# A hybrid attention layer on one Trainium2 core: attention products tied to the emission order of the projection products

## The chip, the cores and the metric

The kernel runs on one core of one Trainium2 chip. The core has a matrix engine (PE, TensorE), three engines for elementwise work (DVE, VectorE; ACT, ScalarE; POOL, GpSimd) and a queue that issues the transfers between memory on and off the chip (SP, SyncE). Each engine takes its instructions in the order in which they stand in the built program. The metric is the time of one execution on the device in microseconds, taken as the median over several runs.

## What is computed

One encoder layer for 1024 positions of width 1024, in float32. A conditioning vector gives shifts, scales and gates. Two groups of eight heads attend side by side, latent attention (MLA) and attention over a band of nine chunks (CA), and a gated MLP follows.

```python
mod = jnp.dot(jax.nn.silu(c), w_ada[l]) + b_ada[l]
sh_a, sc_a, g_a, sh_m, sc_m, g_m = jnp.split(mod, N_MOD, axis=-1)
h = modulate(rmsnorm(x, g_attn_norm[l]), sh_a, sc_a)
proj = jnp.dot(h, w_in[l])
q_lat, kv_lat, k_rope, ca_qkv = jnp.split(proj, split_pts, axis=-1)
q = jnp.dot(rmsnorm(q_lat, g_q_latent[l]), w_q_up[l])
kv = jnp.dot(rmsnorm(kv_lat, g_kv_latent[l]), w_kv_up[l])
...
o_mla = mla_attention(q, k, v)
o_ca = chunk_attention(cq, ck, cv, rel_bias[l])
mixed = jnp.dot(jnp.concatenate([o_mla, o_ca], axis=-1), w_out[l])
x = x + g_a[:, None, :] * mixed
h = modulate(rmsnorm(x, g_mlp_norm[l]), sh_m, sc_m)
u = causal_dwconv(jnp.dot(h, w_up[l]), conv_w[l], conv_b[l])
gate, val = jnp.split(u, 2, axis=-1)
x = x + g_m[:, None, :] * jnp.dot(jax.nn.silu(gate) * val, w_down[l])
```

## The kernel before

A float32 product is made as three products of high and low parts (`gemm3`). The stages are: the normed input, its transposes and the first query and key projection (qk0); the attention stage, in which all other projections and both kinds of attention run side by side; the output projection and the preparation of the MLP; the MLP up, with its convolution; the MLP down. The change touches the attention stage alone.

The attention stage emits two streams of work. The first is the attention itself: 16 CA units (4 head pairs, 2 heads, 2 halves of the queries) and then 16 MLA units. A unit n is worked on in pieces:

- `prep` turns the unit's queries and keys on PE (`turned`, tag T, one PSUM buffer) and ACT and DVE write them as 16-bit high and low pages; it is done two units ahead.
- `guard(j)` (L755, L763) makes the scores of 128 queries once, only to take their extreme with a DVE reduction (L771); `mrow` turns these into a row that is added to the scores later. Both are done one unit ahead.
- `st(x)` (L815) makes the scores of key block x, transposed; ACT takes the exponential (L819), ACT or POOL its high half (L823, L77), DVE the low half (L826).
- `val(x)` (L841 to L843) multiplies these with the values, two blocks later (`DEPTH`), into one PSUM tile for the unit; after the last block ACT and DVE scale the result (L848 to L850) and SP stores it (L851).

The second stream is the filler: generators that make the other projections in the order v0, qk1, qk2, v1, qk3, m, up0, up1, oca. v and qk are the CA values, queries and keys, m the MLA latents, up0 and up1 the latents' projections to heads, oca the output projection of the CA half. `pace` advances the filler by one step for so much attention work. A step of `gemm3_f` (L162) is two pairs, that is six matmuls, or fewer at the end. Its weights come through `load_w` (L177): 16 tiles hold two sets of weights, three raw buffers receive the loads (L188), ACT makes the high half (L75), POOL the low half (L82). For v1 ACT also takes the squares of the raw weights (L191) into a scratch (tag sq, two buffers) that the norm of the queries and keys (L421) uses too. A side stream, `f_ada`, loads blocks of w_ada (L490) and sums them on DVE (L494); it is advanced with the filler and stores three of its gates through a DMA (L504) that waits for ACT's copy (L503).

What is emitted first does not run first: a scheduler places the instructions of each engine when the program is built, by priority and by when it takes their inputs to be ready. `tc.high_priority(offset=...)` raises a block's priority: 400 for prep, guards, rows and scores, 200 for values. `tc.issue_after(ins)` makes every instruction that its block puts on the engine of `ins` stand behind `ins` in that engine's order. It adds no wait on a semaphore. The kernel before uses it in one direction: a filler step stands behind the attention product that was emitted `LAG + 1` entries back (`trail`, to which every guard, score and value block adds its last matmul).

```python
trail.append(last.ins)
...
if len(trail) > LAG:
    with tc.issue_after(trail[-1 - LAG]):
        gemm3(pt, part, i0 == 0, i0 + step >= n)
```

Of the kernel before, what the change touches and what calls it, by code (L numbers as in the profile page):

```python
# [34 lines left out]
HD = 64  # L35
NM = QR + KVR + ROPE
GRP = 2
GSTEP, LAG = 2, 4
DEPTH = 2
OFF_S, OFF_V = 400, 200  # L40
TB = 1
# [21 lines left out]
def layer_kernel(ctx, tc, I, out):  # L63
    nc = tc.nc
    pe, act, dve, pool, sp = nc.tensor, nc.scalar, nc.vector, nc.gpsimd, nc.sync
# [84 lines left out]
    def gemm3(pt, pairs, start=True, stop=True):  # L150

        n = len(pairs)
        for i, (sh, sl, mh, ml) in enumerate(pairs):
            pe.matmul(pt, sh, mh, start=(start and i == 0), stop=False)
            pe.matmul(pt, sh, ml, start=False, stop=False)
            pe.matmul(pt, sl, mh, start=False, stop=(stop and i == n - 1))

    trail = []  # L160

    def gemm3_f(pt, pairs, step=GSTEP):  # L162
        n, w = len(pairs), pt.shape[-1]
        for i0 in range(0, n, step):
            part = pairs[i0:i0 + step]
            if len(trail) > LAG:
                with tc.issue_after(trail[-1 - LAG]):
                    gemm3(pt, part, i0 == 0, i0 + step >= n)
            else:
                gemm3(pt, part, i0 == 0, i0 + step >= n)  # L170
            yield 3 * len(part) * max(107, w / 2.4 + 2.5)


# [188 lines left out]
    for d in range(ND):  # L362
# [11 lines left out]
        for t in range(NT):  # L374
            h, j = divmod(t, 4)
            sl = slice(j * P, (j + 1) * P)
# [347 lines left out]
    class Unit:  # L724
# [14 lines left out]
        def guard(u, j):  # L739
            i = 4 * u.g + j  # L740
            lo = max(0, i - 4) if u.band else 0
            n = (i - lo + 1) * P
            n0 = max(0, min(4, i + 1) - lo) * P
            n1 = n - n0
            c0 = 512 - n0 if n1 else 0
            segs = [(c0, lo * P, n0, 0)] if n0 else []
            if n1:
                segs.append((512, max(lo, 4) * P - 512, n1, 1))
            q = slice(j * P, (j + 1) * P)
            rows = P if u.band else QK  # L750
            with tc.high_priority(offset=OFF_S):
                s = ps.tile([P, 1024], F32, name=f"s{u.nm}_{i}", tag="S", bufs=1)
                last = None
                for x, (c, ko, w, kh) in enumerate(segs):
                    last = pe.matmul(s[:, c:c + w], u.q[:rows, 0, q], kpages[u.nm, kh][:rows, 0, ko:ko + w],  # L755
                                     start=True, stop=True)
                if u.band:
                    bg = biases[u.hd][0]
                    w = min(n, 256)
                    pc = [(c0 + n - w, 256 - w, w)] if (n1 == 0 or n1 >= 256) else \  # L760
                        [(c0 + n - 256, 0, 128), (c0 + n - 128, 128, 128)]
                    for c, bo, w in pc:
                        last = pe.matmul(s[:, c:c + w], identr[:], bg[:, bo:bo + w], start=False, stop=True,  # L763
                                         skip_group_check=True)
                trail.append(last.ins)
                if u.band:
                    if i >= 4:
                        dve.memset(s[64:128, c0:c0 + 64], BIG)
                else:
                    dve.memset(s[0:64, c0 + n - 64:c0 + n], BIG)  # L770
                dve.tensor_reduce(mz[:, QK + j:QK + j + 1], s[:, c0:c0 + n], axis=AX.X, op=MIN)  # L771
            return sum(w / 2.4 + 12 for _, _, w, _ in segs) + (110 if u.band else 0)

        def mrow(u):
            r = u.row
            with tc.high_priority(offset=OFF_S):
                pt = turned(lambda j: mz[:, QK + j - r:QK + j + 1], r + 1, f"mr{u.nm}_{u.g}")
                act.activation(u.q[r:r + 1, u.slot], pt[r:r + 1], AF.Copy, scale=-1.0)  # L778
            return 4 * 110

        def st(u, x):
            b, t0, t1 = u.blocks[x]
            w = (t1 - t0 + 1) * P
            kt = u.kpage(b)
            kc = slice((b % 4) * P, (b % 4 + 1) * P)
            qc = slice((t0 - 4 * u.g) * P, (t0 - 4 * u.g) * P + w)
            nm = f"{u.nm}_{u.g}_{b}"
            r = u.row
            with tc.high_priority(offset=OFF_S):
                if u.first and x == 0:  # L790
                    pool.memset(f32(mk_k[32:33, 0:64]), 0.0)
                    pool.memset(f32(mk_k[0:1, 64:128]), BIG)
                s = ps.tile([P, 512], F32, name=f"t{nm}", tag="ST", bufs=2)
                todo = []
                if u.band:
                    todo.append((0, w, kt[:, 0, kc], u.q[:, 0, qc]))
                    todo.append((0, w, kt[:r + 1, 1, kc], u.q[:r + 1, 1, qc]))
                    if b >= t0:
                        bt = biases[u.hd][1]
                        wb = min(256, w)  # L800
                        todo += [(0, wb, identr[:], bt[:, a, :wb]) for a in range(2)]
                    elif b + 1 >= t0:
                        bt = biases[u.hd][1]
                        todo += [(0, P, identr[:], bt[:, a, P:2 * P]) for a in range(2)]
                    if t1 == b + 4:
                        todo.append((w - P, w, mk_k[:], mk_q[:]))
                else:
                    todo.append((0, w, kt[:r + 1, 0, kc], u.q[:r + 1, 0, qc]))
                    todo.append((0, w, kt[:r, 0, kc], u.q[:r, 1, qc]))
                    todo.append((0, w, kt[:r, 1, kc], u.q[:r, 0, qc]))  # L810
                    if b >= t0:
                        todo.append((0, P, mk_k[:], mk_q[:]))
                todo.append(todo.pop(1))
                for y, (c0, c1, l, m) in enumerate(todo):
                    last = pe.matmul(s[:, c0:c1], l, m, start=(y == 0), stop=(y == len(todo) - 1))  # L815
                trail.append(last.ins)
                ninv = (sca if u.band else scm)[:, 1:2]
                p = at.tile([P, 512], F32, name=f"p{nm}", tag="P", bufs=2)
                act.activation(p[:, :w], s[:, :w], AF.Exp, scale=ninv)  # L819
                hl = at.tile([P, 2, 512], F16, name=f"hl{nm}", tag="HL", bufs=HL_BUFS)  # L820
                cnt[0] += 1
                if HI_ON[cnt[0] % len(HI_ON)] == "a":
                    act.activation(hl[:, 0, :w], s[:, :w], AF.Exp, scale=ninv)  # L823
                else:
                    hi_of("p", hl[:, 0, :w], p[:, :w])
                dve.tensor_tensor(hl[:, 1, :w], p[:, :w], hl[:, 0, :w], op=SUB)  # L826
                u.hl[x] = hl
            return sum(max(107, (c1 - c0) / 2.4 + 12) for c0, c1, _, _ in todo)

        def val(u, x):  # L830
            b, t0, t1 = u.blocks[x]
            w = (t1 - t0 + 1) * P
            c = slice((t0 - 4 * u.g) * P, (t0 - 4 * u.g) * P + w)
            v, y = u.vst(b)
            w1, w2 = (v[:, y, a, u.odd:u.odd + 2].rearrange("p c b -> p (c b)") for a in range(2))
            hl = u.hl.pop(x)
            with tc.high_priority(offset=OFF_V):
                if x == 0:
                    u.pv = ps.tile([P, 512], F32, name=f"pv{u.nm}_{u.g}", tag="pv", bufs=1)
                end = x == len(u.blocks) - 1  # L840
                pe.matmul(u.pv[:, c], w1, hl[:, 0, :w], start=(x == 0), stop=False)  # L841
                pe.matmul(u.pv[:, c], w1, hl[:, 1, :w], start=False, stop=False)
                last = pe.matmul(u.pv[:, c], w2, hl[:, 0, :w], start=False, stop=end)  # L843
                trail.append(last.ins)
                if end:
                    ri = at.tile([P, 512], F32, name=f"ri{u.nm}_{u.g}", tag="ri", bufs=1)
                    r0, r1 = (slice(64, 128), slice(0, 64)) if u.odd else (slice(0, 64), slice(64, 128))
                    act.activation(ri[r0], u.pv[r1], AF.Ln)  # L848
                    act.activation(ri[r0], ri[r0], AF.Exp, scale=-1.0)
                    dve.scalar_tensor_tensor(ri[r0], u.pv[r0], vscale[u.vs][1][r0], ri[r0], op0=MUL, op1=MUL)  # L850
                    sp.dma_start(u.dst_d[:, u.g * 512:(u.g + 1) * 512], ri[r0])  # L851
            return 3 * (w / 2.4 + 3)
# [429 lines left out]
```

## Time and profile before

| | us |
|---|---|
| median of 3 runs | 1508.36 |
| lowest and highest of them | 1503.86, 1509.09 |
| the profiled execution's own time | 1507.0 |
| its span, from the first to the last instruction | 1505.2 |
| PE, DVE, POOL, ACT busy in that span | 1323.0, 1011.6, 818.5, 715.4 |

The profile is of one execution. Rows of stretches give for each engine how long it was busy and, after an x, how many instructions it ran, then the granted clock of PE as a share of full speed, the busy share of the DMA engines and their rate. Rows of groups give line, engine, operation, output and inputs with shapes, the count, the busy time in us and the mean of one in ns, and behind the bar the engine's idle time just before them with what ended it. Rows of events give start and duration in us. A matmul's duration in an event row includes its passage through the array, so that successive ones overlap; what counts is the distance of their starts.

### The profile page before, as it was taken

How to read it: one execution, taken by the hardware profiler on the slowest of the kernel's cores; microseconds unless marked ns; L12 is line 12 of the kernel's file. 1: busy time of each engine (PE TensorE's matmuls, PEld its weight loads, DVE VectorE, ACT ScalarE, POOL GpSimd, SP SyncE). 2: the span in 40 equal slices, each digit the busy share in tenths (PEclk: the TensorE clock that was granted, in tenths of full speed). 3: DMA queues.
4: the chain of work that ended last, by engine and by line, in shares of the span. 5: the costliest groups of instructions: out<-in, count | busy, mean ns of one | idle time of the engine just before them, and what ended most of it. 6: DMA issues, size and time to landing. Idle time of an engine off the chain costs nothing.

```text
span 1505.2 us, 19968 instructions
## 1 busy us (share of the span) xinstructions
PE 1323.0 (88%) x6926; PEld 1054.2 (70%) x6926; DVE 1011.6 (67%) x1421; ACT 715.4 (48%) x1319; POOL 818.5 (54%) x901
## 2 busy tenths in 40 slices
PE   3769999898868899988928759999999999999997
PEld 2769879776745556655716648888888887887885
DVE  8926665555667866565676668777777888666563
ACT  5435565454756766665453324444444433333331
POOL 5764444353698443322867245555556554665662
PEclk9979999999977999999958979999999999999999
DMA  8421223221110023324521142222222234446442
GB/s 308 124 67 50 64 61 111 80 74 43 57 35 8 18 82 98 103 81 149 211 98 56 56 154 84 85 84 84 78 77 84 85 123 172 147 145 231 163 140 98
DMA packets 80001, 153.02 MB, mean 102 GB/s; under 512 B 8214, under 2 KB 44314, under 8 KB 79900
## 3 DMA queue, kind: packets, MB, share of 16 engines
q1 hardware_dynamic: 79900, 151.75, 30.5%
q8 instruction: 54, 0.88, 0.3%
q14 instruction: 47, 0.39, 0.1%
HBM read 122.88 MB, written 28.84 MB: 101 GB/s over the span
## 4 chain that ended last, share of the span: by engine, by line
PE 34%; DVE 18%; POOL 16%; DMA 16%; issue 10%; ACT 5%; DVEq 0%; SPq 0%; POOLq 0%; ACTq 0%
DMA aw<-w_ada 7%; POOL wds L82 4%; DMA wu<-w_up 4%; PE tm L815 3%; DVE u L1132 3%; PE dnp L1196 2%; PE dnp L1197 2%; PE dnp L1198 2%; PE p L1126 2%; PE p L1124 2%; PE p L1125 2%; DVE aacc L494 2%; DVE wu L1154 2%; DVE u L1133 2%; DVE adaw L369 1%
## 5 line engine op out<-in xcount | busy, mean ns | idle before, releaser
L82 POOL TENSOR_TENSOR wds<-wd,wds 128x512 fp32r<-128x512 f32 x88 | 152.9, 1756 | 100.2 <-ACT wds L75 100.2
L75 ACT ACTIVATE wds<-wd 128x512 fp32r<-128x512 f32 x88 | 54.6, 624 | 152.2 <-PE dnp L1198 149.6
L1196 PE MATMUL dnp<-wds,g 128*128 128x512 f32 x308 | 119.7, 390 | 2.3 <-DVE c L1158 1.5
L1186 DVE TENSOR_TENSOR wd<-wd,gmbc 128x1024 f32<-128x1024 f32 x44 | 69.9, 1588 | 76.3 <-DMA wd<-w_down 76.2
L1198 PE MATMUL dnp<-wds,g 128*128 128x512 f32 x308 | 118.5, 390 | 2.2 <-DVE g L82 2.2
L1197 PE MATMUL dnp<-wds,g 128*128 128x512 f32 x308 | 119.7, 389 | 0.0
L82 POOL TENSOR_TENSOR wc<-ws,wc 128x512 fp32r<-128x512 f32 x22 | 55.4, 2520 | 74.2 <-ACT wc L75 74.2
L494 DVE SCALAR_TENSOR_TENSOR aacc<-aw,cs,aacc 128x256 f32<-128x256 f32 x84 | 45.4, 541 | 62.5 <-DMA aw<-w_ada 62.1
L82 POOL TENSOR_TENSOR wa<-wu,wa 128x512 fp32r<-128x512 f32 x22 | 36.7, 1669 | 90.6 <-ACT wa L75 90.6
L815 PE MATMUL tm<-qt,kt 96*128 96x512 f16 (+7 forms) x288 | 74.1, 346 | 7.7 <-ACT qt L778 4.7
L826 DVE TENSOR_TENSOR hlm<-pm,hlm 128x512 f16<-128x512 f32 (+1 forms) x96 | 58.3, 615 | 32.6 <-POOL hlm L77 17.8
L1132 DVE SCALAR_TENSOR_TENSOR u<-c,pk,u 128x1023 f32<-128x1023 f32 x44 | 75.5, 1724 | 4.1 <-ACT u L1131 4.1
L82 DVE TENSOR_TENSOR g<-gr,g 128x512 fp32r<-128x512 f32 x44 | 70.6, 1607 | 9.9 <-ACT g L75 9.9
L819 ACT ACTIVATE pc<-tc,sca 128x512 f32<-128x512 f32 (+3 forms) x96 | 50.2, 524 | 47.5 <-DVE hlc L826 27.9
L815 PEld LDWEIGHTS <-kt 128*128 128x128 f16 (+2 forms) x480 | 47.4, 102 | 35.2 <-issue 16.8
L77 POOL TENSOR_SCALAR hlm<-pm 128x384 f16<-128x384 f32 (+2 forms) x48 | 24.8, 516 | 82.9 <-ACT pm L819 65.1
L1196 PEld LDWEIGHTS dnp<-wds,g 128*128 128x128 f32 x308 | 57.8, 188 | 15.6 <-ACT wds L75 1.9
L1198 PEld LDWEIGHTS dnp<-wds,g 128*128 128x128 f32 x308 | 57.8, 188 | 15.0 <-DVE g L82 3.0
L819 ACT ACTIVATE pm<-tm,scm 128x512 f32<-128x512 f32 (+1 forms) x96 | 55.3, 579 | 27.2 <-PE tm L815 20.6
L1131 ACT ACTIVATE u<-c,pk 128x1024 f32<-128x1024 f32 x44 | 52.3, 1236 | 32.9 <-DVE c L1164 32.9
L826 DVE TENSOR_TENSOR hlc<-pc,hlc 128x512 f16<-128x512 f32 (+3 forms) x96 | 52.8, 553 | 22.5 <-POOL hlc L77 11.9
L1197 PEld LDWEIGHTS dnp<-wds,g 128*128 128x128 f32 x308 | 57.8, 188 | 11.9
(432 smaller groups left out, 4703.1 us busy)
## 6 DMA issues: line engine op xcount, KB each, us to landing
wu<-w_up SPq DMA_DIRECT2D x44, 512.0 KB, 3.5
wd<-w_down SPq DMA_DIRECT2D x44, 512.0 KB, 3.6
aw<-w_ada SPq DMA_DIRECT2D x96, 128.0 KB, 2.1
g_d<-u SPq DMA_DIRECT2D x22, 512.0 KB, 2.6
gr<-g_d SPq DMA_DIRECT2D x44, 256.0 KB, 2.8
x<-x SPq DMA_DIRECT2D x16, 512.0 KB, 7.1
adaw<-w_ada_a SPq DMA_DIRECT2D x16, 512.0 KB, 5.1
wq_r<-w_qk SPq DMA_DIRECT2D x32, 128.0 KB, 2.4
```

The costliest lines, as they stand in the source:

```text
L75: act.activation(o, i, AF.Copy)
L82: (pool if eng == "p" else dve).tensor_tensor(o, i, f32(hi), op=SUB)
L494: dve.scalar_tensor_tensor(acc[:], w[:], cs[:, k:k + 1], acc[:], op0=MUL, op1=ADD)
L815: last = pe.matmul(s[:, c0:c1], l, m, start=(y == 0), stop=(y == len(todo) - 1))
L819: act.activation(p[:, :w], s[:, :w], AF.Exp, scale=ninv)
L826: dve.tensor_tensor(hl[:, 1, :w], p[:, :w], hl[:, 0, :w], op=SUB)
L1131: act.activation(u[:], c, AF.Identity, scale=pk[:, cv + 2:cv + 3], bias=pk[:, cv + 3:cv + 4])
L1132: dve.scalar_tensor_tensor(u[:, 1:], c[:, :S - 1], pk[:, cv + 1:cv + 2], u[:, 1:], op0=MUL, op1=ADD)
L1186: dve.tensor_tensor(raw[:], raw[:], gmbc[:], op=MUL)
L1196: pe.matmul(pts[t][n], sh, w[n][:, 0], start=(j == 0), stop=False)
L1197: pe.matmul(pts[t][n], sh, w[n][:, 1], start=False, stop=False)
L1198: pe.matmul(pts[t][n], sl, w[n][:, 0], start=False, stop=(j == NF - 1))
```

## The change

A second list, `ftrail`, keeps the last matmul of each filler step (`gemm3` returns it). A helper, `behind`, opens the block of an attention piece: it raises the priority by `OFF_S`, and if more than `FLAG` = 6 filler steps have been emitted, the block's matmuls stand behind the last matmul of the filler step that was emitted seven entries back. Guards, rows, scores and values use it. The values' priority offset becomes 400 in place of 200 with it. `prep` keeps its old block, and filler steps keep theirs.

```diff
-GSTEP, LAG = 2, 4
+GSTEP, LAG, FLAG = 2, 4, 6
...
-            pe.matmul(pt, sl, mh, start=False, stop=(stop and i == n - 1))
+            last = pe.matmul(pt, sl, mh, start=False, stop=(stop and i == n - 1))
+        return last.ins
...
-    trail = []
+    trail, ftrail = [], []
+
+    def behind(stack):
+        stack.enter_context(tc.high_priority(offset=OFF_S))
+        if len(ftrail) > FLAG:
+            stack.enter_context(tc.issue_after(ftrail[-1 - FLAG]))
...
                 with tc.issue_after(trail[-1 - LAG]):
-                    gemm3(pt, part, i0 == 0, i0 + step >= n)
+                    ftrail.append(gemm3(pt, part, i0 == 0, i0 + step >= n))
             else:
-                gemm3(pt, part, i0 == 0, i0 + step >= n)
+                ftrail.append(gemm3(pt, part, i0 == 0, i0 + step >= n))
...
-            with tc.high_priority(offset=OFF_S):
+            with ExitStack() as sk:
+                behind(sk)
                 s = ps.tile([P, 1024], F32, name=f"s{u.nm}_{i}", tag="S", bufs=1)
...
-            with tc.high_priority(offset=OFF_S):
+            with ExitStack() as sk:
+                behind(sk)
                 pt = turned(lambda j: mz[:, QK + j - r:QK + j + 1], r + 1, f"mr{u.nm}_{u.g}")
...
-            with tc.high_priority(offset=OFF_S):
+            with ExitStack() as sk:
+                behind(sk)
                 if u.first and x == 0:
...
-            with tc.high_priority(offset=OFF_V):
+            with ExitStack() as sk:
+                behind(sk)
                 if x == 0:
                     u.pv = ps.tile([P, 512], F32, name=f"pv{u.nm}_{u.g}", tag="pv", bufs=1)
```

## The prediction

> **What bounds the kernel now.** I read the page first (busy shares, then the slices), next the time in stretches cut at marks of the filler work, and last the order of events at two of these marks. The page:
>
> ```profile
> span 1505.2 us, 19968 instructions
> ## 1 busy us (share of the span) xinstructions
> PE 1323.0 (88%) x6926; PEld 1054.2 (70%) x6926; DVE 1011.6 (67%) x1421; ACT 715.4 (48%) x1319; POOL 818.5 (54%) x901
> ...
> PE   3769999898868899988928759999999999999997
> ...
> PEclk9979999999977999999958979999999999999999
> ```
>
> PE is the engine to watch, but it is not full everywhere: slices 11 and 12 (414 to 489 us) hold 6 and 8 tenths at 0.7 of the clock. That is inside the attention stage, the only stage that the change touches. I number the projection products ("fills") as PE issues them: qk0 is 1 to 192, v0 to 384, qk1 to 576, qk2 to 768, v1 to 960, qk3 to 1152, m to 1344, up0 to 1416, up1 to 1488, oca to 1680. The stretches below begin at fill 373, at the first of v1 (769), at v1's first fill behind its last weight tile (about 793), at the first of m (1153), at m's second set of transposes, at up0's scale, at up1's scale, and at fill 1453.
>
> ```profile
> core 0: us, PE busy (x) PEld busy (x) DVE busy (x) ACT busy (x) POOL busy (x), PEclk, DMA share, GB/s
> 120.80:211.80 91.00, 87.78 (x697) 79.38 (x695) 58.41 (x114) 48.76 (x96) 40.42 (x60) 1.00 0.21 62
> 211.80:230.70 18.90, 16.38 (x114) 12.33 (x112) 14.07 (x29) 16.49 (x46) 9.65 (x15) 0.91 0.22 65
> 230.70:305.90 75.20, 69.33 (x548) 63.44 (x548) 43.35 (x102) 36.32 (x78) 30.43 (x45) 1.00 0.33 96
> 305.90:385.00 79.10, 70.84 (x441) 58.42 (x439) 42.52 (x86) 44.55 (x121) 39.85 (x102) 0.96 0.19 56
> 385.00:404.00 19.00, 15.60 (x105) 11.46 (x104) 13.32 (x28) 14.48 (x33) 10.72 (x24) 0.91 0.23 65
> 404.00:454.70 50.70, 37.97 (x167) 25.40 (x166) 35.47 (x88) 29.22 (x67) 43.84 (x84) 0.80 0.13 36
> 454.70:472.30 17.60, 16.53 (x84) 12.44 (x85) 11.78 (x35) 11.63 (x27) 14.53 (x34) 0.81 0.04 8
> 472.30:701.90 229.60, 204.88 (x1126) 130.92 (x1124) 152.58 (x296) 155.49 (x290) 91.51 (x136) 0.95 0.22 70
> ```
>
> Until 305.9 us PE is busy 92 to 96% of the time outside the short second stretch: there a matmul more or less is time. From 404 to 454.7 us POOL leads with 43.84 of 50.7 us (86%), and PE idles 12.7 us.
>
> **The change, part by part.** No instruction is added, removed or resized; only orders move. In the built order of the changed program 3497 of PE's 8149 places hold another instruction, and places on ACT, DVE, POOL and SP change with it; from fill 1465 on PE's order differs only by a few places. Scores, guards, row transposes and values may now stand at most six filler steps ahead of the filler; values also rise from the lower to the higher priority. Head preparations keep their old rule. Counting the attention matmuls that stand ahead of a given fill, before and after: at 769, 421 and 360; at 793, 506 and 365; at 1153, 686 and 597; at 1345, 1034 and 911; at 1417, 1118 and 1100; at 1465, 1213 in both. So attention is pushed back behind the projections, by up to 141 matmuls, and all of it comes back before fill 1465. The question is what stands beside it where it left and where it returns.
>
> (a) *120.8 to 211.8.* 61 matmuls leave. The stretch's mean is 87.78/697 = 0.126 us, PE is 96% busy: -7.7 us. Bounds -8.0 (all the way at the price of the wall clock, 91.0/697 = 0.131) and -4 (waits between scores and guards stay and half of the gain with them).
>
> (b) *211.8 to 230.7: v1's weights.* The start of v1 is a gate, and here is its chain. The last qk2 product issues, its PSUM is copied and squared, the scratch of that square comes free for v1's weights, these load through three buffers, and POOL makes the last low half just before the fill that needs it:
>
> ```profile
> 211.37 0.28 PE L156 MATMUL ipq<-wq_s,hT 128*128 128x256 f32 x1
> ```
> ```profile
> 213.24 0.61 ACT L419 ACTIVATE raw<-ipq 128x512 f32<-128x512 f32 x1
> ...
> 214.37 0.62 ACT L421 ACTIVATE sq<-raw 128x512 f32<-128x512 f32 x1
> ...
> 217.91 0.41 ACT L191 ACTIVATE wv_j<-wv_r 128x256 f32<-128x256 f32 x1
> ```
> ```profile
> 229.88 0.73 POOL L82 TENSOR_TENSOR wv_s<-wv_r,wv_s 128x256 fp32r<-128x256 f32 x1
> ```
> ```profile
> 230.67 0.38 PE L155 MATMUL ipv<-wv_s,hT 128*128 128x256 f32 x1
> ```
>
> From 211.65 to 230.61 us the chain takes 19.0 us, and before it is covered by 85 attention matmuls. After, 5 stand between fills 769 and 793: 29 matmuls at 0.126, 3.7 us, and the rest is bare waiting, because the scores that could run stand behind a fill that waits. But the chain itself gets shorter: ACT, 16.49 us busy of 18.9 there, and POOL lose the softmax in between. The eight weight tiles pass three buffers, so the last load waits for a buffer that an earlier tile leaves:
>
> ```profile
> wv_r<-w_v SPq DMA_DIRECT2D x16, 128.0 KB, 2.3
> ```
>
> Bounds for the chain: 18.9 us (not shortened), and 8.1 us with nothing queued: copy and square 1.23, then twice a load, a high half (as long as the 0.41 above) and a low half, 2 x (2.3 + 0.41 + 0.73). I take 13, between, since ACT, POOL and SP still queue other work there: -5.9, bounds -10.8 and 0.
>
> On SP these loads stand behind loads of w_ada, and those behind a store that waits for ACT's copy of a gate:
>
> ```profile
> SPq L504 <- ACT gab L503: 11.0, 1, 11.0
> ```
>
> The changed order moves attention outputs and biases back past them by up to 41 places, so v1's weights are not later for SP's sake. If an output that comes later now stalls the queue, w_ada loads and weights behind it wait, which the bounds of (b) and (d) hold.
>
> (c) *230.7 to 305.9.* 52 of the matmuls return (141 fewer becomes 89 fewer) in a stretch that is 92% busy: 52 x 69.33/548 = 6.6 us. Bounds 0.7 (the idle 5.9 us takes the rest) and 7.1 (at the wall clock, 0.137).
>
> (d) *305.9 to 404: m.* 34 more leave, at 70.84/441 = 0.161: 5.5 us. But m has gates of its own (its last weights, and its transposes, which wait for POOL's norms) that shorter cover lays bare, as in (b). I take half, -3; bounds -5.5 and +3 (the gain is lost and as much again waits).
>
> (e) *404 to 454.7: up0.* 105 matmuls return between fills 1345 and 1417, 84 becoming 189. At the 0.161 of (d) that is 16.9 us of PE into 12.7 us of idle, at the stretch's own slow 37.97/167 = 0.227, 23.8 us. What comes with them matters more. Between up0's and up1's first sum of squares DVE's order holds 33 instructions more (net): 10 subtractions of the low half, 10 guard reductions, 6 memsets, two head pages, two final scalings, and three of other work.
>
> ```profile
> L826 DVE TENSOR_TENSOR hlc<-pc,hlc 128x512 f16<-128x512 f32 (+3 forms) x9 | 5.7, 632 | 1.8 <-POOL hlc L77 1.4 <-ACT hlc L823 0.4
> ...
> L771 DVE TENSOR_REDUCE mz<-sm 128x1 f32<-128x128 f32 (+3 forms) x4 | 1.9, 479 | 0.0
> L771 DVE TENSOR_REDUCE mz<-sc 128x1 f32<-128x640 f32 x2 | 1.6, 816 | 0.0
> L850 DVE SCALAR_TENSOR_TENSOR ric<-pvc,vabc,ric 64x512 f32<-64x512 f32 x2 | 1.5, 747 | 0.0
> ...
> L890 DVE SCALAR_TENSOR_TENSOR qt<-mq_ps,scm,qt 96x512 f16<-96x512 f32 x1 | 0.7, 741 | 0.0
> L770 DVE MEMSET sm<- 64x64 f32 x4 | 0.4, 112 | 0.4 <-PE sm L755 0.3
> ```
>
> 10 x 0.632 + 10 x 0.65 (between the two reductions) + 6 x 0.112 + 2 x 0.747 + 2 x 0.741 = 16.5 us. DVE then has 35.47 + 16.5 = 52.0 us to do in a stretch of 50.7, and it becomes the bound there. At 100% that is +1.3 us; at the 86% that the leading engine reaches in this stretch 52.0/0.86 = 60.4, +9.7. I take +8, near the second: on all engines up0's own steps hang on each other. Bounds 0 and 23.8.
>
> The row's clock is 0.80 here. [...]
>
> (f) *472.3 to the end of attention.* PE's order there differs mainly in values that move up before a score or a filler. A value waits for its softmax a little longer, and what it passed runs later. Price +1; bounds -1 and +4, at most a quarter of a us for each of the sixteen units, below the waits that this row shows already:
>
> ```profile
> L815 PE MATMUL tm<-qt,kt 97*128 97x512 f16 x48 | 19.8, 415 | 7.5 <-ACT qt L778 4.7 <-ACT pm L819 2.4 <-ACT hlm L823 0.4
> ```
>
> The MLP (from 900 us) keeps its order: 0.
>
> **Sum:** -7.7 - 5.9 + 6.6 - 3 + 8 + 1 = -1.0. The profiled execution took 1507.0 us, so 1506.0; that execution lies 0.1% under the median of the runs shown, so 1507. My forecast is no change: what the early stretches gain by doing less attention, up0 pays back. Its own range, with (b) and (e) moved by some 5 us each way, is 1499 to 1516.
>
> **Rivals.**
> *Slower: up0 pays in full.* Fills of up0 and scores now wait for each other in both directions, every drain of up0 queues behind softmax on DVE, and PE stays at its slow rate: (e) is 23.8 us, the rest as above. Sum +14.8, 1522. For it: DVE's 52.0 us do not fit, and POOL is at 86% already. Against it: PE has 12.7 us of idle time there. It decides once (e) exceeds 16.5 us (9.0 gained in the other terms, and 7.5 to be seen).
> *Faster: up0 hides it.* (e) is 1.3, (d) -5.5, (f) 0: sum -11.2, 1496 against the profiled execution, 1497 against the median. For it: idle on PE, and attention matmuls that need no drain of up0. Against it: the same DVE sum.
> *The order binds nothing,* because the scheduler would place the work alike: excluded for the most part by the 3497 moved places; what is left is an order that differs where nothing waits. 1508.
>
> **How the numbers follow.** Differences under 0.5% (7.5 us) can't be told from none in these runs. Forecast 0.38 (of it 0.27 within, 0.05 faster, 0.06 slower), full payment 0.35 (slower), hiding 0.23 (faster), no effect 0.04 (same). Together faster 0.28, same 0.31, slower 0.41; the slower rival outweighs the faster one because DVE's sum already lies over the stretch. The range reaches to both: 1491 (hiding, with (a) and (b) at their better bounds) to 1528 (full payment with (b) unshortened), leaving out about 2 in 10.
>
> **What would show it.** In the profile after: a bare PE wait of about 10 us at v1's start, ended by POOL's low half (b); v1's first fill some 8 us earlier, m's start some 7 us earlier (a to c); up0 to up1 longer than 50.7 us, with DVE above 85% (e); the MLA part as long as before within 4 us (f). If PE has no bare wait at v1, (b) is wrong; if up0's stretch stays at 50 us, the faster rival holds; if it passes 67 us, the slower one. A loss that sits in the MLA part or at an SP wait for an attention output would make the whole account wrong.

## The result, and the profile after

| | before | after |
|---|---|---|
| median, us | 1507.74 (17 runs) | 1515.96 (17 runs) |
| lowest and highest, us | 1503.79, 1515.07 | 1511.73, 1522.5 |
| ratio after / before | | 1.0055, 95% interval 1.004 to 1.0069 |
| span of the profiled execution, us | 1505.2 | 1513.7 |

The change makes the kernel 0.55% slower. That is small, but it is more than the 0.5% that the prediction took for the limit of what can be told, and the forecast of no change was wrong by 9 us; the time lies at the upper end of the forecast's own range (1499 to 1516 us).

Line numbers of the changed kernel are 6 to 10 higher than before (scores L824, guards L762 and L770, values L851 to L853, transposes L707). The page of the changed kernel:

```profile
span 1513.7 us, 19961 instructions
...
PE 1320.8 (87%) x6926; PEld 1053.9 (70%) x6926; DVE 1014.2 (67%) x1421; ACT 716.5 (47%) x1319; POOL 820.3 (54%) x901
...
PE   3779989889777899988937849999999999999997
...
PEclk9979989999998999998967969999999999999999
```

PE does the same work in the same busy time (1320.8 us against 1323.0). Slices 11 and 12 (counted from 0) held 6 and 8 tenths before and now hold 7 and 7: the hole there has become wider and shallower, and it begins earlier, with slice 10, which had 8 and has 7. The profile cut at the same fills as in the prediction (373, 769, 793, 1153, 1345, 1417, 1465, 1681); columns as there: length, then busy time and instructions by engine, then the granted clock:

```profile
core 0: us, PE busy (x) PEld busy (x) DVE busy (x) ACT busy (x) POOL busy (x), PEclk, DMA share, GB/s
119.30:204.10 84.80, 80.70 (x651) 73.84 (x650) 49.83 (x97) 44.09 (x88) 39.93 (x55) 1.00 0.22 65
204.10:218.00 13.90, 7.57 (x33) 5.72 (x32) 4.85 (x12) 7.91 (x27) 7.59 (x11) 0.69 0.24 76
218.00:303.90 85.90, 78.55 (x598) 70.16 (x598) 51.24 (x113) 41.85 (x88) 31.58 (x51) 0.97 0.31 88
303.90:403.50 99.60, 82.79 (x518) 67.13 (x517) 52.71 (x108) 56.41 (x148) 49.19 (x124) 0.95 0.18 54
403.50:463.80 60.30, 46.34 (x262) 33.09 (x263) 45.96 (x111) 40.14 (x89) 49.48 (x94) 0.90 0.13 36
463.80:497.80 34.00, 28.54 (x163) 21.10 (x164) 28.42 (x69) 24.22 (x54) 28.78 (x58) 0.93 0.04 9
497.80:711.30 213.50, 192.35 (x1066) 121.59 (x1064) 140.27 (x267) 146.20 (x270) 77.60 (x111) 0.96 0.24 76
```

For m (fills 1153 to 1345) and for up0 with up1's start (1345 to 1465) the kernel before, cut at its own times of these fills, has:

```profile
305.90:405.10 99.20, 87.54 (x553) 70.76 (x550) 56.73 (x116) 59.09 (x154) 50.87 (x126) 0.95 0.20 58
...
405.10:489.80 84.70, 67.00 (x303) 45.09 (x302) 60.23 (x152) 51.43 (x115) 74.59 (x148) 0.80 0.09 24
```

The length of each stretch, before and after, from the profiles above and from a second, later pair of profiles of the same two kernels (experiments h1 and h2):

| fills | before | after | difference | second pair | difference |
|---|---|---|---|---|---|
| start to 373 | 121.0 | 119.3 | -1.7 | 121.4, 118.9 | -2.5 |
| 373 to 769 | 90.9 | 84.8 | -6.1 | 90.1, 88.3 | -1.8 |
| 769 to 793, v1's weights | 19.0 | 13.9 | -5.1 | 19.0, 13.9 | -5.1 |
| 793 to 1153 | 74.9 | 86.0 | +11.1 | 73.7, 85.4 | +11.7 |
| 1153 to 1345, m | 99.2 | 99.5 | +0.3 | 98.9, 101.6 | +2.7 |
| 1345 to 1465, up0 and up1's start | 84.7 | 94.3 | +9.6 | 83.5, 94.9 | +11.4 |
| 1465 to 1681 | 214.3 | 213.5 | -0.8 | 215.0, 210.8 | -4.2 |
| 1681 to the end | 801.1 | 802.4 | +1.3 | 802.7, 801.8 | -0.9 |

So the changed kernel is ahead by 13 us (9 in the second pair) when v1's first full step runs, has almost nothing of that left when m starts (2 us ahead; in the second pair 2 us behind), gains nothing in m, and pays 10 us in up0 and up1's start. Three places matter.

*Behind v1's weights.* What PE waits for in the gate (us in total, times, longest), and the two stretches of 4 us behind it:

```profile
PE ipv L154 <- ACT wv_s L75: 3.9, 1, 3.9
PE ipv L155 <- POOL wv_s L82: 2.3, 3, 1.4
```

```profile
218.00:222.00 4.00, 4.00 (x20) 3.91 (x20) 0.81 (x6) 1.58 (x4) 2.73 (x5) 0.50 0.33 102
222.00:226.00 4.00, 4.00 (x31) 3.47 (x30) 0.94 (x2) 2.36 (x6) 2.87 (x6) 0.86 0.39 121
```

The gate is bare: 6.3 us of idle PE in 13.9. PE comes out of it at half the clock: 20 matmuls in the first 4 us, 31 in the next. In units of the full clock these 8 us lose 4 x 0.50 + 4 x 0.14 = 2.6 us.

*In m.* PE's waits above 1.5 us in m's first half (up to fill 1249) and its second, and then the longest of them beside the order of DVE (start, length, engine, line, operation, and in brackets the idle time before it and what ended it):

```profile
PE k_ps L707 <- DVE qt L878: 6.0, 1, 6.0
...
PE p_ada L513 <- DVE latT L572: 3.2, 1, 3.2
PE sc L762 <- DVE mz L778: 2.0, 2, 1.4
```

```profile
342.77 1.06 PE L707 MATMUL k_ps<-ident,qn 128*64 128x128 f32 x4 [6.01 <-DVE qt L878]
...
336.25 0.48 DVE L500 SCALAR_TENSOR_TENSOR aacc<-aw,cs,aacc 128x256 f32<-128x256 f32 x1 [1.95 <-DMA aw<-w_ada]
336.65 0.74 DVE L860 SCALAR_TENSOR_TENSOR ric<-pvc,vabc,ric 64x512 f32<-64x512 f32 x1
338.94 0.48 DVE L500 SCALAR_TENSOR_TENSOR aacc<-aw,cs,aacc 128x256 f32<-128x256 f32 x1 [1.55 <-DMA aw<-w_ada]
339.35 0.42 DVE L778 TENSOR_REDUCE mz<-sc 128x1 f32<-128x256 f32 x1
341.64 0.48 DVE L500 SCALAR_TENSOR_TENSOR aacc<-aw,cs,aacc 128x256 f32<-128x256 f32 x1 [1.87 <-DMA aw<-w_ada]
342.04 0.68 DVE L878 SCALAR_TENSOR_TENSOR qt<-q_ps,qt 64x512 f16<-64x512 f32 x1
```

The query's low half (L878) stands in DVE's order behind sums of w_ada (L500), and each of these waits for its own transfer, one in 2.7 us. DVE idles, PE waits 6.0 us for the PSUM buffer that L878 reads, and all that is behind it on PE waits too. In m as a whole 35 matmuls fewer make PE 4.75 us less busy (87.54 to 82.79), and its idle time grows from 11.66 to 16.81 us.

*In up0.* The stretch from 403.5 to 463.8 us is 10.5 us longer than before's 405.1 to 454.9 (60.3 against 49.8). DVE is busy 45.96 of 60.30 us there, 76%, and POOL 82%: neither is full. DVE has 10.5 us more to do there than in the kernel before (35.47), not the 16.5 that the prediction added up.

### The profile page after: what moved, and what is told of

The parts are those of the page before. It is cut to its first block, busy times and chain, and to the rows that moved or that the text cites. A ratio compares the mean times of both kernels' runs of the same rounds, so it can differ in the third digit from the quotient of the medians.

```text
span 1513.7 us, 19961 instructions
## 1 busy us (share of the span) xinstructions
PE 1320.8 (87%) x6926; PEld 1053.9 (70%) x6926; DVE 1014.2 (67%) x1421; ACT 716.5 (47%) x1319; POOL 820.3 (54%) x901
## 4 chain that ended last, share of the span: by engine, by line
PE 53%; DVE 15%; DMA 12%; POOL 10%; issue 6%; ACT 3%; DVEq 0%; SPq 0%; POOLq 0%; ACTq 0%
PE p L1136 6%; PE p L1134 6%; PE p L1135 6%; DMA aw<-w_ada 6%; PE dnp L1208 4%; PE dnp L1206 4%; PE dnp L1207 4%; PE tm L824 3%; DMA wu<-w_up 2%; DVE aacc L500 2%; DVE u L1142 1%; DVE u L1143 1%; DVE adaw L375 1%; PE tc L824 1%; PE op L156 1%
## 5 line engine op out<-in xcount | busy, mean ns | idle before, releaser
L82 POOL TENSOR_TENSOR wc<-ws,wc 128x512 fp32r<-128x512 f32 x22 | 52.0, 2366 | 67.3 <-ACT wc L75 67.3
L500 DVE SCALAR_TENSOR_TENSOR aacc<-aw,cs,aacc 128x256 f32<-128x256 f32 x84 | 44.4, 529 | 65.4 <-DMA aw<-w_ada 64.7
L824 PE MATMUL tm<-qt,kt 96*128 96x512 f16 (+7 forms) x288 | 72.2, 341 | 5.5 <-ACT qt L786 3.6
L824 PEld LDWEIGHTS <-kt 128*128 128x128 f16 (+2 forms) x480 | 46.3, 101 | 37.7 <-issue 19.4
L835 DVE TENSOR_TENSOR hlc<-pc,hlc 128x512 f16<-128x512 f32 (+3 forms) x96 | 52.6, 551 | 25.4 <-POOL hlc L77 14.7
L1143 DVE SCALAR_TENSOR_TENSOR u<-c,pk,u 128x1022 f32<-128x1022 f32 x44 | 64.8, 1507 | 0.0
```

What stands on the lines that cost most here:

```text
L82: (pool if eng == "p" else dve).tensor_tensor(o, i, f32(hi), op=SUB)
L1143: dve.scalar_tensor_tensor(u[:, 2:], c[:, :S - 2], pk[:, cv:cv + 1], u[:, 2:], op0=MUL, op1=ADD)
```

## The experiments

The kernels of one group ran on one chip, with the kernel before beside them, and every ratio is to that; the 95% interval stands in parentheses. Chips and single executions differ (the medians of the kernel before lie between 1507.74 and 1514.42 us, and fills 373 to 769 of the changed kernel took 84.8 and 88.3 us in its two profiles), so that a difference of two or three us between stretches of two kernels says little. "Left" in the table at the end of this section is the number of attention matmuls that the built order leaves behind m's last product for up0 and up1.

### Which part of the change, and where: e1_prio, e2_lock, e3_v1open, e4_lateopen

e1_prio is the kernel before with only the values' priority changed:

```diff
-            with tc.high_priority(offset=OFF_V):
+            with tc.high_priority(offset=OFF_S):
```

> The kernel before with one edit: values get the priority offset 400 in place of 200; no order rule. Theory T (the order rule costs: attention pushed behind the filler leaves the filler's gates bare and comes back where it is dear): no loss, 1504 to 1511 us, since attention stands no later in PE's order than before (505 attention matmuls ahead of fill 793 against 506, 1073 ahead of 1345 against 1034). Rival R1 (the values' priority costs: values stand before their softmax is done): the whole loss, about 1516 us, with longer PE waits of values.

Measured: 0.994 (0.9919 to 0.9961), *faster* than before, where R1 expected the whole loss.

e2_lock is the changed kernel with the values back at the lower priority (`behind` takes the offset as an argument):

```diff
-                behind(sk)
+                behind(sk, OFF_V)
```

> The changed kernel with values back at offset 200, the order rule kept. T: as the changed kernel, 1514 to 1518 us, with the bare wait at v1 (PE's order up to fill 1345 has the same counts of attention matmuls). R1: as before, about 1508 us. Rival R2 (only the pile-up at up0 costs): as the changed kernel too.

Measured: 1.0066 (1.0043 to 1.0089). The loss belongs to the order rule: with the rule in force, the values' priority makes no difference that can be told.

e3_v1open lifts the rule at v1's first twelve filler steps (steps counted from v0's first), e4_lateopen at those of m, up0, up1 and the first eight of oca:

```diff
-            stack.enter_context(tc.issue_after(ftrail[-1 - FLAG]))
+            i = len(ftrail) - 1 - FLAG
+            stack.enter_context(tc.issue_after(ftrail[95 if 96 <= i < 108 else i]))
```

> The changed kernel, but attention that would be tied to one of v1's first 12 filler steps is tied to the last step of qk2, so that it may pass v1's gate. 403 attention matmuls ahead of fill 793 against 365 in the changed kernel (506 before). T: 38 matmuls cover about 5 of the 9 us of bare wait and PE's clock is kept: 1509 to 1513 us, the gain visible between fills 769 and 865 and kept to the end. R2 (only up0's pile-up costs): no change at the end, 1515 to 1517, because the counts at 1153 and 1345 are those of the changed kernel.

Measured: 1.0053 (1.0032 to 1.0074), as slow as the changed kernel. Up to m the edit did what it should. Behind the gate the clock is full again (1.00) and the stretch has before's length, 75.9 us. About half of the 10 us that it is shorter than in the changed kernel is 35 matmuls that had already run before it (563 against 598, at 0.126 us 4.4). But up0 and up1's start still take 97.8:

```profile
221.90:297.80 75.90, 70.96 (x563) 63.96 (x562) 44.41 (x99) 37.15 (x79) 30.15 (x44) 1.00 0.32 91
400.30:498.10 97.80, 75.33 (x424) 53.87 (x425) 74.80 (x183) 63.85 (x142) 80.82 (x157) 0.89 0.09 25
```

e4_lateopen has `ftrail[159 if 160 <= i < 224 else i]` in that line.

> The changed kernel, with the order rule lifted for attention that would be tied to a filler step of m, up0 or up1 (tied to the last step of qk3 instead). 967 attention matmuls ahead of fill 1345 against 911 (1034 before). R2: the loss goes, about 1508 us. T: part of it, as m's and up0's waits get half of their cover back: 1510 to 1513 us, the bare wait at v1 unchanged.

Measured: 0.9966 (0.9951 to 0.9982), 0.9% below the changed kernel's ratio and faster than before, although up to m's start attention is pushed back as far as in the changed kernel but for 12 matmuls. Its m has no such wait for transposes: PE idles 6.65 us in 91.6, with 44 matmuls more than the changed kernel's m.

```profile
308.40:400.00 91.60, 84.95 (x562) 71.53 (x561) 56.00 (x120) 61.57 (x159) 51.14 (x126) 1.00 0.21 59
400.00:490.80 90.80, 71.96 (x369) 49.89 (x368) 71.63 (x170) 59.29 (x133) 78.73 (x155) 0.87 0.10 25
```

### Is it the loads of w_ada? f1_aw5_before, f2_aw5_after, f3_mopen, f4_upopen

The 6.0 us wait suggested a theory (H): the sums of w_ada, paced by their loads, hold DVE, and the rule keeps PE from going around them. Two kernels give these loads five buffers instead of three, in the kernel before and in the changed one; two others lift the rule in m alone and in up0 and up1 alone.

```diff
-        return apg.tile([P, 256], F32, name=name, tag="A", bufs=3)
+        return apg.tile([P, 256], F32, name=name, tag="A", bufs=5)
```

> The kernel before with five instead of three buffers for the loads and running sums of w_ada. Theory H (the sums of w_ada on DVE, each waiting for one load at a time, hold up everything that stands behind them on DVE): the loads run ahead, DVE's idle time before these sums falls from about 62 us to under 30, and the kernel is 0.3 to 0.6% faster than before. Rival U (the loss sits in the pile of softmax work at up0 and not at these sums): within 0.2% of before.

Measured: 0.9847 (0.9824 to 0.9871). This is the best version of the study that computes the layer, 1.5% faster than before.

> The changed kernel with the same five buffers. H: the wait of PE for the key transposes behind DVE's query step (6.0 us in the changed kernel's m) is gone, and the ratio to before falls from 1.0055 to at most 1.002. U: the ratio stays at 1.004 to 1.007, and the time from up0's start to its end stays about 10 us above before.

Measured: 0.9962 (0.9947 to 0.9977), but the wait for the key transposes is still 4.7 us. DVE's wait for these loads over the whole span, in f1 and then in f2 (total, times, longest; before 62.1 and after 64.7 us):

```profile
DVE aacc L494 <- DMA aw<-w_ada: 33.4, 35, 2.4
```

```profile
DVE aacc L500 <- DMA aw<-w_ada: 36.6, 34, 2.5
```

H expected the buffers to help the changed kernel more than the kernel before. They help it less (0.9% against 1.5%), and the distance between the two grows to 1.2%. The pacing loads cost both kernels; they are not what the rule mainly pays for.

f3_mopen and f4_upopen have `ftrail[159 if 160 <= i < 192 else i]` and `ftrail[191 if 192 <= i < 224 else i]`.

> The changed kernel with the rule lifted only for attention that is tied to the filler steps of m; up0 and up1 keep it. H: most of the 0.9% that lifting it for m, up0 and up1 together gave comes back here, ratio to before 0.997 to 1.000, and the 6.0 us wait in m is gone. U: 1.004 to 1.007.

Measured: 0.9988 (0.9972 to 1.0004), and no wait for key transposes above 0.2 us.

> The changed kernel with the rule lifted only for attention that is tied to the filler steps of up0 and up1; m keeps it. H: 1.003 to 1.006, the 6.0 us wait in m stays. U: most of the gain comes from here, 0.997 to 1.001, and the time from up0's start to its end falls by 6 to 10 us against the changed kernel.

Measured: 1.0024 (1.0008 to 1.004), with a wait of 6.2 us in m. Of the 0.9% of e4_lateopen, lifting in m gives 0.7 and lifting in up0 and up1 0.3. For m the stretches agree: m with up0 and up1's start takes 186.0 us in f3, against 193.8 in the changed kernel (196.6 in h2). For up0 and up1 they do not: these stretches take 197.5 us in f4, since the 56 matmuls that leave them run in m, and m grows by 7 us while up0 and up1's start shrink by 3. Where the 0.3% of f4 comes from is not shown.

### The loads taken away, and the distance changed: g1_oneload_before, g2_oneload_after, e5_flag24, f7_aw5_prio

g1 and g2 leave out seven of every eight loads of w_ada, so that they do not compute the layer; their sums on DVE are as many as before.

```diff
-                    w = atile(f"aw{m}_{n}_{k}")
-                    sp.dma_start(w[:], I["w_ada"][k * P:(k + 1) * P, c0:c0 + 256])
                     if k == 0:
+                        w = atile(f"aw{m}_{n}_{k}")
+                        sp.dma_start(w[:], I["w_ada"][k * P:(k + 1) * P, c0:c0 + 256])
```

> The kernel before with only the first of every eight loads of w_ada: the other seven are left out and their sums read the first tile again (so the gates and scales that come of w_ada are others), with DVE's sums as many as before. It is the base for the next run, and has about the 1.5% that more buffers gave, or more: 0.975 to 0.987 of before.

Measured: 0.9846 (0.9821 to 0.9871).

> The changed kernel with the same seven of eight loads left out. If the loads that pace DVE are what the rule pays for, the 6.0 us wait of PE for the key transposes in m shrinks to under 2 us and the ratio of this run to the same cut of the kernel before is at most 1.003. If the rule costs at up0 and at v1 by itself, whatever DVE waits for, the ratio of the two stays at 1.005 to 1.012, as it was with five buffers.

Measured: 0.988 (0.9859 to 0.9902), 0.35% above g1, between the two expectations. The wait for the key transposes did shrink, as the first of them said; g2's waits and its m, then g1's m:

```profile
PE k_ps L707 <- DVE qt L878: 0.9, 1, 0.9
```

```profile
293.70:383.80 90.10, 81.02 (x518) 66.42 (x516) 54.34 (x107) 56.51 (x149) 52.34 (x124) 0.99 0.11 29
```

```profile
297.20:388.20 91.00, 84.62 (x552) 69.67 (x549) 59.40 (x113) 58.41 (x153) 52.56 (x124) 0.98 0.09 25
```

So the loads do make that wait, but m without them is 9 us shorter in the changed kernel and 8 us shorter in the kernel before, which waits for the same loads at other points. The 0.35% that remains is less than the 0.55%, but the intervals of g1 and g2 overlap, so these two alone do not say whether the loads have a small part in the difference. With f2, where the distance grew, H is out as the main cause.

e5_flag24 keeps attention 24 filler steps back instead of six (`FLAG = 24`).

> The changed kernel with attention held 24 filler steps back instead of six. Ahead of m's last product stand 1070 attention matmuls instead of 911, so 48 instead of 189 are left for up0. Volume theory (every attention matmul that is left for up0 costs about 0.10 us there, and the late matmuls are what the change pays): up0 takes 45 to 48 us instead of 60, m takes 97 to 102, ratio to before 0.993 to 0.999. Tie theory (filler and attention that are tied to each other in both directions cost wherever it is): at least 1.003.

Measured: 1.0018 (1.0003 to 1.0034). Half of the volume theory's numbers hold: up0 takes 47.5 us, and up0 with up1's start 80.4, *below* before's 84.7, with the rule in force. But m takes 110.8, not 97 to 102, and the ratio lies between the two expectations:

```profile
307.20:418.00 110.80, 98.73 (x601) 78.55 (x599) 62.68 (x129) 63.73 (x164) 56.21 (x132) 0.94 0.19 52
418.00:498.40 80.40, 60.23 (x267) 41.65 (x266) 58.60 (x141) 47.18 (x107) 72.86 (x142) 0.79 0.08 22
418.00:465.50 47.50, 34.86 (x123) 23.69 (x122) 32.30 (x75) 24.96 (x58) 41.94 (x82) 0.68 0.11 32
```

What does not stand in up0 stands in m, and is paid there.

f7_aw5_prio is e1_prio with five buffers.

> The kernel before with the values at the higher priority and five buffers for w_ada, without the rule. If the two gains add up, 0.9847 x 0.994 = 0.979 of before; if more buffers already take what the priority gave, 0.984 to 0.986.

Measured: 0.9974 (0.9956 to 0.9992): the two gains do not add, and with five buffers the priority *costs* 1.3% (0.9974 against 0.9847). Its gain with three buffers is thus no property of the priority, but of the order that came out.

### The gate itself: f5_both, e6_junk_before, e7_junk_after, g3_late_aw5

f5_both joins e3 and e4 (v1 and the late steps):

```diff
-            stack.enter_context(tc.issue_after(ftrail[-1 - FLAG]))
+            i = len(ftrail) - 1 - FLAG
+            i = 95 if 96 <= i < 108 else 159 if 160 <= i < 224 else i
+            stack.enter_context(tc.issue_after(ftrail[i]))
```

> The changed kernel with the rule lifted at v1's first twelve filler steps and at all steps of m, up0 and up1. If the gain at v1 was real and only swallowed later by the ties in m and up0, it adds to the 0.9% of e4_lateopen: m starts about 10 us earlier than there and the ratio to before is 0.989 to 0.993. If attention that is done early at v1 only moves waits (the matmuls cost the same wherever they stand), the ratio stays at 0.995 to 0.998.

Measured: 0.9944 (0.9927 to 0.9961), between the two expectations.

e6 and e7 take away the gate's cause: the scratch of the square goes into a tile that is overwritten right behind it, so that v1's weights need not wait for it. v0's weights take the same path (they are squared too), and up to fill 373 both kernels are 2 us shorter (118.8 and 117.4 us against 121.0 and 119.3). So it is not the gate at v1 alone that the edit changes.

```diff
-                    junk = qtile(f"{name}j{k}")
-                    act.activation(junk[:, :c.stop - c0], rw, AF.Square, accum_out=ssw[:, k:k + 1])
+                    act.activation(hi[:, c], rw, AF.Square, accum_out=ssw[:, k:k + 1])
```

> The kernel before with the square's scratch written into the tile of the high half that is overwritten right behind it, so that v1's weights need not wait for the scratch. The gate at v1 was covered in the kernel before, so it gains little: 0.996 to 1.000.

Measured: 0.9968 (0.9955 to 0.9982).

> The changed kernel with the same edit. The bare wait at v1 (6.3 us of idle PE and the 2.6 us of slow clock behind it) should shrink to 2 us or less. If the gate's price counts at the end, the ratio to before falls from 1.0055 to 0.998 to 1.001; if what is won there is lost in m and up0, as with e3_v1open, it stays at 1.003 to 1.006.

Measured: 0.997 (0.9953 to 0.9986). With the gate gone the two kernels are equal (medians 1508.87 and 1509.45 us): the whole loss of 0.55% has disappeared. The ratio lies a little below the first expectation, because the kernel before gains 0.3% by the same edit. Gate, stretch behind it, and up0 with up1's start in e7:

```profile
206.10:211.10 5.00, 4.64 (x41) 4.19 (x39) 4.15 (x9) 3.65 (x9) 2.43 (x3) 1.00 0.55 152
211.10:294.50 83.40, 76.53 (x591) 68.32 (x590) 52.84 (x116) 40.40 (x84) 31.84 (x50) 0.98 0.28 78
397.40:494.10 96.70, 77.94 (x424) 54.49 (x425) 77.39 (x184) 63.98 (x142) 81.54 (x157) 0.87 0.10 25
```

From v1's first fill to m's start it takes 88.4 us, the changed kernel 99.8. Up0 still pays as in the changed kernel: 96.7 us, against 81.3 in e6. So the rule's gain and its price are both there, and without the bare gate they cancel in the medians. In the profiled executions, of which e7's was 3.7 us above its median, e7 is 9.1 us ahead of e6 at m's start and 4.6 us behind it at the end.

g3_late_aw5 is e4_lateopen with five buffers for w_ada.

> The changed kernel with the rule lifted in m, up0 and up1 (as e4_lateopen) and five buffers for w_ada. Two separate costs: the gains add, 0.9966 x 0.9907 = 0.987 of before. One cost: no better than the better of the two, 0.995 to 0.997.

Measured: 0.9923 (0.9907 to 0.9938): better than either edit alone on the changed kernel, less than the sum, and behind f1_aw5_before, which has no rule at all.

### Both kernels again: h1_before_here, h2_after_here

> The kernel before, unchanged, on the chip of the experiments: ratio 1 within 0.2%. By the account so far: v1's weights 17 to 19 us, m 96 to 102 us, the stretch of up0 and up1's start 81 to 86 us with 304 attention matmuls.

> The changed kernel, unchanged, on the same chip: ratio 1.004 to 1.008. By the account: v1's weights 13 to 14 us, the stretch behind them 86 us, m as long as in the kernel before within 3 us though 34 fewer attention matmuls stand there, the stretch of up0 and up1's start 94 to 100 us with 425. If m comes out 5 us or more shorter than before's here, m's waits are no part of the loss.

Measured: 1.0 (0.9982 to 1.0018) and 1.006 (1.004 to 1.008). M and then up0 with up1's start, in h1 and in h2, and the first 4 us behind the gate in h2:

```profile
304.20:403.10 98.90, 86.80 (x553) 69.71 (x550) 57.48 (x116) 59.12 (x154) 50.08 (x126) 0.97 0.20 58
403.10:486.60 83.50, 64.53 (x302) 43.27 (x301) 61.20 (x153) 51.77 (x117) 74.91 (x148) 0.82 0.09 24
```

```profile
306.50:408.10 101.60, 84.73 (x517) 68.26 (x515) 52.40 (x107) 56.49 (x148) 49.58 (x123) 0.94 0.18 53
408.10:503.10 95.00, 75.51 (x424) 53.94 (x425) 73.83 (x181) 64.24 (x142) 79.18 (x153) 0.90 0.10 26
...
221.10:225.10 4.00, 4.00 (x21) 3.91 (x20) 0.81 (x6) 1.49 (x4) 2.72 (x5) 0.50 0.31 100
```

The pair repeats the first one's differences for the gate, the stretch behind it, and up0 with up1's start within 2 us, and the half clock too. The early gain up to fill 769 is smaller (4.3 us instead of 7.8), m is 2.7 us longer instead of 0.3, and fills 1465 to 1681 are 4.2 us shorter instead of 0.8.

### All kernels side by side

| kernel | ratio | v1's gate | behind it | m | left | up0 and up1's start |
|---|---|---|---|---|---|---|
| before | 1 | 19.0 | 74.9 | 99.2 | 179 | 84.7 |
| e1_prio | 0.994 | 17.2 | 84.7 | 95.0 | 140 | 79.7 |
| f1_aw5_before | 0.9847 | 17.5 | 72.9 | 97.3 | 179 | 81.9 |
| f7_aw5_prio | 0.9974 | 14.7 | 86.5 | 98.0 | 140 | 80.9 |
| g1_oneload_before | 0.9846 | 16.4 | 70.2 | 91.0 | 172 | 82.3 |
| e6_junk_before | 0.9968 | 4.4 | 89.6 | 103.1 | 172 | 81.3 |
| e5_flag24 | 1.0018 | 16.5 | 82.2 | 110.8 | 144 | 80.5 |
| g3_late_aw5 | 0.9923 | 12.7 | 83.8 | 100.1 | 232 | 85.1 |
| f5_both | 0.9944 | 16.0 | 81.8 | 100.1 | 246 | 86.6 |
| e4_lateopen | 0.9966 | 14.0 | 87.0 | 91.6 | 246 | 90.8 |
| f4_upopen | 1.0024 | 14.1 | 87.2 | 106.4 | 246 | 91.1 |
| after | 1.0055 | 13.9 | 86.0 | 99.5 | 302 | 94.3 |
| f2_aw5_after | 0.9962 | 12.8 | 82.9 | 100.3 | 303 | 96.2 |
| e7_junk_after | 0.997 | 5.0 | 83.4 | 102.9 | 302 | 96.6 |
| g2_oneload_after | 0.988 | 12.8 | 75.0 | 90.1 | 303 | 96.7 |
| f3_mopen | 0.9988 | 14.1 | 87.9 | 89.1 | 302 | 96.9 |
| e3_v1open | 1.0053 | 15.6 | 75.9 | 102.6 | 302 | 97.7 |
| e2_lock | 1.0066 | 13.4 | 86.1 | 100.6 | 302 | 100.0 |

The last two columns go together: a straight line through these and the second pair of profiles, 20 in all, is 64.4 us + 0.105 us for each attention matmul left, and leaves 1.7 us of scatter. So up0 and up1's start follow what is left for them, with few waits for loads or many. Whether the rule by itself costs there is harder to part from this: every kernel with 302 or 303 left has the rule in force there, and only e5_flag24 has it, at a longer distance, with as few as 144. M has no such line.

## Why the prediction was right and wrong

(a) *Right in kind, the size open.* 61 matmuls fewer were to give -7.7 from fill 373 on. Some of them leave before that fill: the stretch itself holds 46 fewer (651 against 697) and gave -6.1 in the first pair and -1.8 in the second, which is outside the bound of -4. From the start to fill 769 it is -7.8 and -4.3.

(b) *Right in its size and its kind.* The gate was to shorten by 5.9 and to lie bare for some 10 us, ended by POOL's low half. It shortened by 5.1 in both pairs. The bare wait was shorter, 6.3 us of idle PE, and most of it was ended by ACT's high half (3.9), the rest by POOL's low half (2.3).

(c) *The first step that failed: a term mis-sized, outside its bounds.* Predicted +6.6 (0.7 to 7.1), measured +11.1 and +11.7. 51 more matmuls at the predicted 0.126 are 6.4. What was missing is the gate's own tail: 2.6 us of withheld clock (0.50 for 4 us and 0.86 for 4 us, behind a gate with a wait of 3.9 us) and 1.5 us more idle time (7.35 against 5.87). The prediction had taken the stretch's clock, 1.00, as given. With (a) and (b) as they came out, m started 2.0 us earlier in the first pair and 2.3 us later in the second, not some 7 us earlier. Where the gate was covered or gone, the clock behind it stayed at 1.00 (e3) and 0.98 (e7). The clock in up0 rose (0.80 to 0.90), but up0 was 10.5 us longer all the same.

(d) *The second step that failed.* "I take half, -3": 34 matmuls left m, PE was 4.75 us less busy, and all of it became waiting: +0.3 and +2.7. The largest piece is the 6.0 us wait of a head's transposes for DVE's L878; the waits for m's last weights and for POOL's norms, which the prediction named, are not among the long ones. e4_lateopen and f3_mopen, which let attention go around that wait, have an m of 91.6 and 89.1 us; but f5_both, without the wait too (1.1 us at most), has 100.1, so what sets m's length stays open. The bounds (-5.5 to +3) held the result, the choice between them was wrong.

(e) *Right in size by luck, for the wrong reason.* +8 predicted for up0; measured +10.6 and +10.7 for up0 (fills 1345 to 1417), +9.6 and +11.4 with up1's start. But DVE did not become the bound: it got 10.5 us more to do, not 16.5, and was busy 76%, not above 85%. What the 20 profiles show instead is a length that goes with the volume, 0.105 us for each attention matmul left. 123 more (302 instead of 179) make 12.9 by that line, close to the measured two. Nothing of it went into PE's idle time: 12.7 us before, 14.0 after.

(f) *Nothing there*, as nearly predicted (+1): +0.5 from fill 1465 on in the first pair. In the second it was -5.1, below the bound of -1; no cause was found.

From the predicted -1.0 to the measured +8.5 it is thus 4.5 us in (c), 3.3 in (d), 1.6 in (e) and 0.1 in the rest. In the second pair, 11.3 us in all, the misses are 5.1 in (c), 5.7 in (d) and 3.4 in (e) by the same count, (a) gave 3.4 less than predicted, and (f) 6.1 more. Of the rivals, "up0 pays in full" was slower too, but by another way: up0 took 60.3 us and not 67. "Up0 hides it" is refuted by the same 60.3, and "the order binds nothing" by the stretches up to fill 1465. The prediction gave 0.41 to slower and 0.31 to no change.

A reading that fits these: an attention matmul costs about as much where it leaves (0.126 up to fill 769 in the first pair, though 4.3 us for 61 is only 0.07 in the second) as where it comes back (0.126 behind v1, 0.105 in up0), so that moving it gains nothing by itself. What is left is the waits that the move lays bare or covers. The runs support this without settling it. That the order rule makes the loss is shown (e2 keeps it, e1 does not have it). With the gate's cause gone, e7 and e6 are equal; but e3_v1open covers the gate in another way and keeps the whole loss, so the gate alone does not explain it. Lifting the rule at the late steps takes the loss away (e4, and in m alone f3).

Open is how these go together. The edits of the changed kernel that help and still compute the layer recover 0.3 to 1.3% of its time, the larger ones more than the change cost, and they do not add: e3_v1open reaches m's start 6 us before the changed kernel's first profile and 9 us before its second, and has the changed kernel's ratio; f5_both lifts the rule in m like e4_lateopen, and its m is 100.1 us, not 91.6. Every edit reshuffles the order of all engines, and the length of m (89 to 111 us) follows no single number that was tried.

## What to carry to other kernels

Where an engine is busy nine tenths of the time, moving its work to another stage gained little here but the waits that disappeared, so price the cover that goes with the work: here a bare gate cost its wait (6.3 us of idle PE) and then 4 us at half the clock (0.50). An order rule in both directions can take away the way around a wait, and its price can show at waits that have nothing to do with it, as here behind sums paced by single loads (one in 2.7 us, and a wait of 6.0 us). And with a static order a gain of half a per cent may belong to the order that came out and not to the edit: try it again with one other thing changed, as the priority here, which gained 0.6% and then cost 1.3%.

## What was not expected of the hardware

The part from fill 1872 on (behind the attention stage), which no edit is aimed at and which has as many matmuls in both, takes 753.7 us in f5_both and 759.2 in e6_junk_before, on the same chip and at the same granted clock:

```profile
751.70:1505.40 753.70, 679.13 (x2952) 554.43 (x2950) 530.22 (x429) 282.44 (x417) 424.11 (x264) 0.95 0.34 112
```

```profile
747.40:1506.60 759.20, 682.47 (x2952) 556.56 (x2949) 531.52 (x429) 282.41 (x417) 427.78 (x264) 0.95 0.34 111
```

The two profiles of the kernel before differ by 1.8 us there (753.2, and 755.0 in h1). 5.5 us are two thirds of the effect studied here; where they come from was not tried.
